# Two feed-forwards in split FP32: TensorE's written order at a part's end, and two adaLN steps moved behind up

## The chip, the cores and the metric

One core of one Trainium2 chip runs the whole program. The metric is the device time of one execution in microseconds. TensorE (PE; its weight loads are PEld) multiplies into PSUM; VectorE (DVE) and ScalarE (ACT) move and change data; GpSimd (POOL) adds and issues some of the DMAs; SyncE (SP) issues the others.

## The reference, cut to what matters

The model is one step of two layers over 640 tokens (512 latent, 128 context) of width 1024. Each layer has a token mixer (attention, then a recurrent unit) and a SwiGLU feed-forward of inner width 2816 = 22 x 128. The shift, scale and gate vectors of both (adaLN) come from a conditioning vector.

```python
def _swiglu(x, w_gu, w_down):
    gate, up = jnp.split(x @ w_gu, 2, axis=-1)
    return (jax.nn.silu(gate) * up) @ w_down

# per layer, after the mixer
f_l = _swiglu(_modulate(lat, norm_g[i, 1], sh2_l, sc2_l), ffn_w_gu[i], ffn_w_down[i])
lat = lat + g2_l[:, None, :] * f_l
```

## The kernel before

Activations lie with the feature on the partitions and the tokens along them, in eight 128-row tiles. Every FP32 operand is split into a high part (rounded, a ScalarE cast) and a low part (the rest, a VectorE subtraction), and a product is three matmuls for each 128-row tile: high x high, high x low, low x high. A planner orders the instructions of each engine: it simulates the program and gives an engine the earliest written instruction that it takes to be ready. `issue_after` puts an instruction behind another one of its engine, and `in_order` makes the chosen engines follow the written order inside its block; instructions from outside may still stand between.

The first feed-forward (`ffn`) works the 22 column blocks f in three parts of 8, 7 and 7. For each f, `ws` makes gate and then up, each in two chunks of tokens (24 matmuls a chunk). Gate's evacuation is L916 and a Silu, up's is L924, a bias step (L927) and the split into `hhi` and `hlo`. A part ends with its down projection (`project`): chunks of 3 matmuls for each f of the part, accumulated over f, and L595 adds each into x. Between, `fill` runs steps of `modulations`, which compute the adaLN vectors of later stages: one step loads 512 KB on POOL's queue (L288) and makes two VectorE products with accumulation (L292), each issued behind the last `self.anchor`. A quota of 56 steps holds for this phase: each gate and each up asks for one (not at f = 0), each chunk pair of the first two down projections for one more. `keep` loads later weights on POOL's queue too, splits them and stores them.

The second feed-forward works on blocks of 4 x 128 features and halves of 320 tokens, with a Strassen-like scheme: seven products for each pair f (gate and up block f) in place of eight, of 12 matmuls each. In the rows they are known by their operands:

- `pair_a(f)`: A11 x B11 (`mx<-big,whi`), copied by ScalarE to `snap`; then A12 x B21 (`mm<-big,whi`).
- `pair_b(f)`: S2 x T2 into the same mx bank (`mx<-big,whx`), copied to `snap` as u2; S1 x T1 (`mc<-big,whx`); S3 x T3 again into the mx bank, which has to wait for u2, and is copied as u3.
- `pair_c(f)`: A22 x T4 into the mx bank (`mx<-xt,wuh`), behind the copy u3; S4 x B22 into the mc bank (`mc<-big,whx`). Then `hidden` multiplies gate and up and splits the result.

`opening` ends the layer before, makes the first two pairs plainly (L1008) and the sums T1 to T4 and their halves (`sums`, `lows`: L1032, L1037) on VectorE, all in written order. `ffn_halves` then goes through six parts of 3, 3, 4, 4, 4 and 4 pairs; the first part's first two pairs are the opening's. The loop writes pair_a(f), pair_c(f - 1), pair_b(f). At a part's end it writes pair_a of the next part's first pair, pair_c, and the down projection (`project_part`), whose weights pass through the same three `raw` and three `whi` buffers as the gate weights. `gate_weights` loads and splits the gate block, `sum_weights` makes S1 to S4 on GpSimd and splits them.

Of the kernel before, what the change touches and what calls it, by code (L numbers as in the profile page):

```python
# [23 lines left out]
CHB = ((320, 642), (0, 320))  # L24
# [4 lines left out]
NF = FF // P  # L29
# [7 lines left out]
ORDERED = (mybir.EngineType.PE, mybir.EngineType.DVE, mybir.EngineType.Activation)  # L37
C0 = 516
FG = (1, 1, 1)
# [95 lines left out]
def _pieces(t0, t1):  # L135
    return [(s, max(a, t0), min(b, t1)) for s, a, b in ((0, 0, NLAT), (1, NLAT, NTOK)) if max(a, t0) < min(b, t1)]


class _Step:
# [761 lines left out]
    def ffn(self, l, hi, lo, fp, last):  # L901
        nc = self.nc
        f0 = 0
        todo = [k for f in range(KT) for k in [("wi", f + KT), ("wi", f)] + [("wg", f // 2)] * (1 - f % 2)] + [("wlo", f) for f in range(KT)]
        todo += [("gu", c * NF + f) for f in range(PLAIN) for c in range(2)] + [("gu", PLAIN)]
        for ci, n in enumerate((8, 7, 7)):
            hhi = self.big()
            hlo = self.big()
            sg = {}

            def eg(j):
                def ev(t0, s, ps):
                    if t0:
                        sg[j] = self.t([P, NTOK], F32, "sg", 2, fp)
                    g = sg[j]
                    self.anchor = nc.vector.tensor_tensor(g[:, s], ps, self.rt[:, s], ALU.mult).ins  # L916
                    for c, a, b in _pieces(s.start, s.stop):
                        nc.scalar.activation(g[:, a:b], g[:, a:b], AF.Silu, bias=self.bias[:, c:c + 1])
                return ev

            def eu(j):
                def ev(t0, s, ps):
                    u = self.t([P, 320], F32, "up", 2, fp)
                    nc.vector.tensor_tensor(u, ps, self.rt[:, s], ALU.mult)  # L924
                    for c, a, b in _pieces(s.start, s.stop):
                        g = sg[j][:, a:b]
                        nc.vector.scalar_tensor_tensor(g, u[:, a - t0:b - t0], self.bias[:, c:c + 1], g, ALU.add, ALU.mult)  # L927
                    self.mark = self.split(hhi[:, j, s], hlo[:, j, s], sg[j][:, s])
                    self.anchor = self.mark[1]
                return ev  # L930
            for j in range(n):
                f = f0 + j
                self.ws(self.i["gu"][l, f], hi, lo, eg(j), FG[0] * (f > 0), CHB)
                self.ws(self.i["gu"][l, NF + f], hi, lo, eu(j), FG[1] * (f > 0), CHB)
                self.keep(todo, KEEP[ci][j])
            w = self.i["dn"][l, :, :, f0:f0 + n]
            if ci == 2:
                last(w, hhi, hlo, (l, 5))
            else:
                def between(f, n=DOWN[ci]):  # L940
                    self.fill(FG[2])
                    self.keep(todo, n[f])
                self.project(w, hhi, hlo, (l, 5), done=between)
            f0 += n
# [307 lines left out]
    def ffn_halves(self, l, q):  # L1252
        self.wx, self.share = 0, False
        qs = [None] * PLAIN + [q]
        f0 = 0
        for ci, n in enumerate(CHN):
            for j in range(n):
                f = f0 + j
                if f < PLAIN:
                    continue  # L1260
                if f == len(qs):
                    qs.append(self.gate_weights(l, f))
                    self.pair_a(qs[f])
                if j and f > PLAIN:
                    self.sum_weights(qs[f])
                    self.pair_c(qs[f - 1])
                    self.last_weights(qs[f])
                self.pair_b(qs[f], j)
            w = self.i["dn"][l, :, :, f0:f0 + n]
            f0 += n  # L1270
            if f0 < NF:
                qs.append(self.gate_weights(l, f0))
                self.pair_a(qs[f0])
            self.pair_c(qs[f])
            if f0 == NF:
                self.share = True
                self.project_last(w, self.hhi, self.hlo, (l, 5))
            else:
                self.sum_weights(qs[f0], ci == 0)
                self.last_weights(qs[f0])  # L1280
                self.project_part(w, self.hhi, self.hlo, (l, 5))
# [398 lines left out]
```

## Time and profile before

| | |
|---|---|
| median of 3 runs | 1485.97 us (1485.88 to 1487.15) |
| the profiled execution | 1488.96 us, span 1487.1 |
| mean granted TensorE clock | 0.996 |
| busy: PE, DVE, ACT, POOL | 1471.2, 1075.0, 728.3, 247.9 us |
| first feed-forward, about | 370 to 840 us |
| second feed-forward, about | 1035 to 1480 us |

The span runs from the first to the last instruction. A busy TensorE is not TensorE at its peak: a matmul of 320 columns shows as 0.31 us, while the next one starts 0.147 us after it, so that two overlap. What counts for the time is the distance from start to start.

### The profile page before, as it was taken

The page shows a single profiled execution, that of the slowest core. Times are in us where ns is not written, and L with a number is a line of the kernel's source. Part 1 is how long each engine was busy: PE and PEld are TensorE (multiplying, and loading weights), DVE is VectorE, ACT ScalarE, POOL GpSimd, SP SyncE. Part 2 cuts the span into 40 slices and gives each one's busy share as a digit, 9 for nine tenths or more (in the row PEclk, how much of TensorE's full clock was granted, in tenths as well). Part 3 has the DMA queues.
Part 4 walks back from the last instruction along what each step waited for, and adds up shares of the span by engine and source line. Part 5 has one row for each costly group of instructions (what it writes and reads, how often), then busy time and mean ns, then how long its engine had stood idle before and what let it go on. Part 6 is the DMA issues. An engine that isn't in the chain of part 4 may idle for free.

```text
span 1487.1 us, 26372 instructions
## 1 busy us (share of the span) xinstructions
PE 1471.2 (99%) x10377; PEld 1440.2 (97%) x10377; DVE 1075.0 (72%) x2054; ACT 728.3 (49%) x1345; POOL 247.9 (17%) x325
## 2 busy tenths in 40 slices
PE   9999999999999999999999999999999999999997
PEld 5999999999999999999999999999999999999997
DVE  6788887875678788887876489985865666565545
ACT  5676666754333234322434298864634343424344
POOL 0001000000012222211210001112032322222311
PEclk9999999999999999999999999999999999999999
DMA  9555555443359899886863744267242131313121
GB/s 371 179 151 172 170 151 155 126 157 100 114 177 323 299 358 326 305 264 218 306 221 125 252 142 142 86 236 247 81 132 86 57 114 57 114 57 109 52 68 71
DMA packets 86026, 255.35 MB, mean 172 GB/s; under 512 B 9056, under 2 KB 22544, under 8 KB 85776
## 3 DMA queue, kind: packets, MB, share of 16 engines
q1 hardware_dynamic: 59152, 157.06, 32.3%
q0 software_dynamic: 26576, 96.49, 18.8%
q8 instruction: 81, 1.33, 0.4%
q14 instruction: 41, 0.34, 0.1%
q10 hardware_dynamic: 176, 0.13, 0.0%
HBM read 206.18 MB, written 43.53 MB: 168 GB/s over the span
## 4 chain that ended last, share of the span: by engine, by line
PE 79%; DMA 8%; DVE 5%; issue 3%; ACT 3%; POOL 1%; DVEq 0%; ACTq 0%; POOLq 0%
PE mm L253 11%; PE mm L255 11%; PE mm L254 11%; PE mx L253 4%; PE mx L255 4%; PE mx L254 4%; PE mx L1203 3%; PE mx L1204 3%; PE mx L1205 3%; DMA mraw<-in_wm 2%; PE op L888 2%; PE gp L1412 2%; PE tp L806 2%; PE mc L1204 1%; PE mc L1203 1%
## 5 line engine op out<-in xcount | busy, mean ns | idle before, releaser
L253 PE MATMUL mm<-big,whi 128*128 128x320 f32 (+3 forms) x1010 | 311.0, 311 | 1.9 <-ACT big L1529 1.8
L254 PE MATMUL mm<-big,whi 128*128 128x320 f32 (+3 forms) x1010 | 312.7, 310 | 0.3 <-DVE big L1530 0.3
L255 PE MATMUL mm<-big,wlo 128*128 128x320 f32 (+3 forms) x1010 | 312.2, 310 | 0.0
L292 DVE SCALAR_TENSOR_TENSOR mprod<-mraw,csb 128x1024 f32<-128x1024 f32 x160 | 194.7, 1217 | 19.6 <-DMA mraw<-in_wm 19.4
L253 PEld LDWEIGHTS mm<-big,whi 128*128 128x128 f32 x1010 | 189.6, 189 | 4.0 <-ACT big L1529 2.4
L254 PEld LDWEIGHTS mm<-big,whi 128*128 128x128 f32 x1010 | 190.5, 189 | 1.7 <-DVE big L1530 0.5
L255 PEld LDWEIGHTS mm<-big,wlo 128*128 128x128 f32 x1010 | 190.1, 189 | 1.0
L1529 ACT CAST whi<-raw 128x1024 fp32r<-128x1024 f32 (+2 forms) x103 | 105.3, 1024 | 143.7 <-PE mm L254 89.6
L1530 DVE TENSOR_TENSOR wlo<-raw,whi 128x1024 fp32r<-128x1024 f32 (+2 forms) x103 | 127.4, 1238 | 33.4 <-ACT whi L1529 33.1
L254 PE MATMUL mm<-big,whx 128*128 128x320 f32 (+3 forms) x443 | 137.4, 310 | 0.0
L255 PE MATMUL mm<-big,wlx 128*128 128x320 f32 (+3 forms) x443 | 137.2, 310 | 0.0
L253 PE MATMUL mm<-big,whx 128*128 128x320 f32 (+3 forms) x443 | 137.0, 310 | 0.0
L595 DVE SCALAR_TENSOR_TENSOR x<-mm,G,x 128x320 f32<-128x320 f32 (+3 forms) x202 | 81.1, 435 | 55.9 <-PE mm L255 50.7
L253 PE MATMUL mx<-big,whi 128*128 128x320 f32 (+3 forms) x318 | 99.2, 312 | 0.0
L255 PE MATMUL mx<-big,wlo 128*128 128x320 f32 (+3 forms) x318 | 98.6, 310 | 0.0
L254 PE MATMUL mx<-big,whi 128*128 128x320 f32 (+3 forms) x318 | 98.4, 310 | 0.0
L288 POOL DMA_DIRECT2D mraw<-in_wm x80 | 42.9, 536 | 317.1 <-DVE mprod L292 203.9
L255 PEld LDWEIGHTS mm<-big,wlx 128*128 128x128 f32 x443 | 83.6, 189 | 0.0
L254 PEld LDWEIGHTS mm<-big,whx 128*128 128x128 f32 x443 | 83.5, 189 | 0.0
L253 PEld LDWEIGHTS mm<-big,whx 128*128 128x128 f32 x443 | 83.4, 188 | 0.0
L1530 DVE TENSOR_TENSOR wlx<-sum,whx 128x1024 fp32r<-128x1024 f32 x40 | 50.2, 1254 | 38.5 <-ACT whx L1529 38.5
L218 ACT CAST kwh<-mraw 128x1024 fp32r<-128x1024 f32 x33 | 34.7, 1051 | 75.6 <-DMA kwi<-kwh 27.7
(396 smaller groups left out, 3886.5 us busy)
## 6 DMA issues: line engine op xcount, KB each, us to landing
raw<-in_gu SPq DMA_DIRECT2D x84, 512.0 KB, 3.6
mraw<-in_wm POOLq DMA_DIRECT2D x80, 512.0 KB, 5.3
raw<-in_dn SPq DMA_DIRECT2D x24, 512.0 KB, 3.7
sw<-in_wm SPq DMA_DIRECT2D x16, 512.0 KB, 10.1
raw<-in_wqk SPq DMA_DIRECT2D x16, 512.0 KB, 4.4
mraw<-in_wi POOLq DMA_DIRECT2D x16, 512.0 KB, 6.4
kwi<-kwh POOLq DMA_DIRECT2D x16, 512.0 KB, 6.3
kwi<-kwl POOLq DMA_DIRECT2D x16, 512.0 KB, 5.4
```

The costliest lines, as they stand in the source:

```text
L218: nc.scalar.copy(high, raw)
L253: nc.tensor.matmul(ps, hi[:, k], xhi[:, k, s], start=(k == 0), stop=False)
L254: nc.tensor.matmul(ps, hi[:, k], xlo[:, k, s], start=False, stop=False)
L255: nc.tensor.matmul(ps, lo[:, k], xhi[:, k, s], start=False, stop=(k == nk - 1))
L288: nc.gpsimd.dma_start(w, self.i["wm"][l * 6 + j - 2, f])
L292: nc.vector.scalar_tensor_tensor(prod, w, 1.0, self.csb[:, s], ALU.mult, ALU.mult, accum_out=out[:, s, f:f + 1])
L595: last = self.nc.vector.scalar_tensor_tensor(xs, ps[:, a - t0:b - t0], G[:, s, f:f + 1], xs, ALU.mult, ALU.add).ins
L1203: nc.tensor.matmul(ps, hi[:, k], xh[:, k], start=start and k == 0, stop=False, skip_group_check=not start)
L1204: nc.tensor.matmul(ps, hi[:, k], xl[:, k], start=False, stop=False, skip_group_check=not start)
L1205: nc.tensor.matmul(ps, lo[:, k], xh[:, k], start=False, stop=(k == KH - 1), skip_group_check=not start)
L1529: high = self.nc.scalar.copy(hi, v).ins
L1530: return high, self.nc.vector.tensor_tensor(lo, v, hi.bitcast(F32), ALU.subtract).ins
```

## The change

In the first feed-forward, the last pair of a part (j == n - 1) asks for no adaLN step after gate and for two after up. In the second one, a part's last pair_b, the next part's first pair_a and the last pair_c are written in this order under `in_order` for TensorE alone, and `gate_weights` of the next part is written ahead of that pair_b.

```diff
             for j in range(n):
                 f = f0 + j
-                self.ws(self.i["gu"][l, f], hi, lo, eg(j), FG[0] * (f > 0), CHB)
-                self.ws(self.i["gu"][l, NF + f], hi, lo, eu(j), FG[1] * (f > 0), CHB)
+                self.ws(self.i["gu"][l, f], hi, lo, eg(j), FG[0] * (f > 0 and j < n - 1), CHB)
+                self.ws(self.i["gu"][l, NF + f], hi, lo, eu(j), (FG[1] + FG[0] * (j == n - 1)) * (f > 0), CHB)
                 self.keep(todo, KEEP[ci][j])
...
                     self.pair_c(qs[f - 1])
                     self.last_weights(qs[f])
-                self.pair_b(qs[f], j)
+                if j < n - 1:
+                    self.pair_b(qs[f], j)
             w = self.i["dn"][l, :, :, f0:f0 + n]
             f0 += n
             if f0 < NF:
                 qs.append(self.gate_weights(l, f0))
-                self.pair_a(qs[f0])
-            self.pair_c(qs[f])
+            with self.in_order(ORDERED[:1]):
+                self.pair_b(qs[f], j)
+                if f0 < NF:
+                    self.pair_a(qs[f0])
+                self.pair_c(qs[f])
             if f0 == NF:
                 self.share = True
                 self.project_last(w, self.hhi, self.hlo, (l, 5))
```

## Rows read from the trace of the kernel before

**Rows 1.** The page: the span, and TensorE's busy time, share and instructions.

```profile
span 1487.1 us, 26372 instructions
PE 1471.2 (99%) x10377; PEld 1440.2 (97%) x10377; DVE 1075.0 (72%) x2054; ACT 728.3 (49%) x1345; POOL 247.9 (17%) x325
```

**Rows 2.** TensorE's waits: line, releaser, us in total, times, longest.

```profile
PE mm L253 <- ACT big L1529: 1.8, 2, 1.4
PE mx L1203 <- ACT snap L1209: 1.4, 3, 0.5
```

**Rows 3.** Timeline of VectorE, first feed-forward, end of part two: start, us, instruction.

```profile
632.96 0.48 DVE L916 TENSOR_TENSOR sg<-mm,r 128x320 f32<-128x320 f32 x1
...
634.36 1.21 DVE L292 SCALAR_TENSOR_TENSOR mprod<-mraw,csb 128x1024 f32<-128x1024 f32 x1
...
635.51 0.48 DVE L924 TENSOR_TENSOR up<-mm,r 128x320 f32<-128x320 f32 x1
635.91 1.21 DVE L292 SCALAR_TENSOR_TENSOR mprod<-mraw,csb 128x1024 f32<-128x1024 f32 x1
...
637.05 0.67 DVE L927 SCALAR_TENSOR_TENSOR sg<-up,bias,sg 128x192 f32<-128x192 f32 x2
```

**Rows 4.** Timeline of TensorE there: idle before it and what ended it, in brackets.

```profile
638.27 0.41 PE L253 MATMUL mm<-big,whi 128*128 128x320 f32 x1 [1.38 <-ACT big L1529]
```

**Rows 5.** Timeline of TensorE, second feed-forward, first part's end (f = 2).

```profile
1070.39 0.31 PE L1008 MATMUL mm<-big,whi 128*128 128x320 f32 x1
...
1074.94 0.31 PE L1203 MATMUL mm<-big,whi 128*128 128x320 f32 x1
...
1078.27 0.41 PE L1203 MATMUL mx<-big,whx 128*128 128x320 f32 x1 [0.52 <-ACT snap L1209]
...
1080.81 0.41 PE L1203 MATMUL mx<-xt,wuh 128*128 128x320 f32 x1 [0.52 <-ACT snap L1209]
...
1082.67 0.31 PE L1203 MATMUL mc<-big,whx 128*128 128x320 f32 x1
```

**Rows 6.** Timeline of VectorE there: the last low halves of T2, then T3.

```profile
1076.35 0.48 DVE L1037 TENSOR_TENSOR big<-c,big 128x320 fp32r<-128x320 f32 x1
1076.76 0.48 DVE L1037 TENSOR_TENSOR big<-x,big 128x320 fp32r<-128x320 f32 x1
```

**Rows 7.** Timeline of TensorE, fourth part's end: first matmuls from S3(12) to S3(13).

```profile
1275.07 0.31 PE L1203 MATMUL mx<-big,whx 128*128 128x320 f32 x1
...
1276.98 0.31 PE L1203 MATMUL mx<-big,whi 128*128 128x320 f32 x1
...
1280.20 0.31 PE L1203 MATMUL mx<-xt,wuh 128*128 128x320 f32 x1
...
1281.97 0.31 PE L1203 MATMUL mc<-big,whx 128*128 128x320 f32 x1
...
1283.73 0.31 PE L1203 MATMUL mx<-big,whx 128*128 128x320 f32 x1
...
1285.77 0.31 PE L253 MATMUL mm<-big,whi 128*128 128x320 f32 x1
...
1286.36 0.31 PE L1203 MATMUL mc<-big,whx 128*128 128x320 f32 x1
...
1288.86 0.31 PE L1203 MATMUL mx<-big,whx 128*128 128x320 f32 x1
```

**Rows 8.** Timeline of ScalarE there: the first down weight's cast, the copy of S2(13).

```profile
1283.69 1.05 ACT L1529 CAST whi<-raw 128x1024 fp32r<-128x1024 f32 x1 [0.54 <-DMA raw<-in_dn]
...
1285.97 0.41 ACT L1209 COPY snap<-mx 128x320 f32<-128x320 f32 x1
```

**Rows 9.** Timeline of TensorE, third part's end: A22(9).

```profile
1214.31 0.42 PE L1203 MATMUL mx<-xt,wuh 128*128 128x320 f32 x1 [0.35 <-ACT snap L1209]
```

**Rows 10.** Stretches near the start: busy time of each engine, granted clock, DMA.

```profile
10.00:15.00 5.00, 4.05 (x31) 2.13 (x30) 3.06 (x5) 1.88 (x4) 0.00 (x0) 1.00 1.03 419
15.00:20.00 5.00, 5.00 (x29) 4.00 (x26) 3.19 (x9) 1.32 (x2) 0.00 (x0) 0.52 1.02 415
20.00:25.00 5.00, 4.93 (x40) 2.97 (x39) 3.02 (x6) 3.82 (x10) 0.00 (x0) 0.80 1.03 410
```

## The prediction

> **What bounds the kernel now.** I read the page first: TensorE is busy for 1471.2 of 1487.1 us [rows 1], so a change that removes no product can gain only what TensorE waits, and loses whenever it makes TensorE wait. Then the table of TensorE's waits: the longest kind is 1.8 us in two waits for a ScalarE cast of `hhi` (first feed-forward), the next 1.4 us in three waits for `snap` (second feed-forward) [rows 2]. Idle under 0.15 us is not listed there. Then TensorE's timeline around each part's end. A wait costs more than the idle figure, because the profile lets a matmul last 0.31 us while the next starts 0.147 us later: twelve matmuls of one product take 1.76 us (1281.97 to 1283.73) [rows 7]. So an idle of 0.52 costs 0.52 + 0.16 = 0.68, and 0.8 with the slow first matmul after it (0.41 instead of 0.31) [rows 5].
>
> **First edit: the adaLN step of the last pair behind up.** A step is one load on POOL's queue and two VectorE products of 1.21 us. The quota of 56 is 14 + 8 + 14 + 8 + 12, so nothing is left for the last pair of the third part, and the edit moves two steps in all: f = 7 and f = 14. At f = 14 both products stand in VectorE's queue between gate and up, at 634.36 and 635.91; up's first evacuation starts at 635.51, and its bias step comes at 637.05 [rows 3]. ScalarE's cast follows that, and TensorE, which has the first six of the seven products of the down projection behind it, starts again at 638.27 after 1.38 us idle [rows 4]. Without the two products the bias step would come 2 x 1.15 = 2.3 us sooner (start to start 1.14 to 1.15), which is more than the wait. Saving: 1.38 + 0.16 = 1.5 us. What is late next: the two products now stand behind up's split, ahead of the residual steps of the down projection, which free PSUM banks; the three mm and two mx banks hold 5 x 3.1 us of chunks (21 matmuls each), so 2.3 us should drain unseen. The load buffer of the moved step comes free later, and with it the next load on POOL's queue, which also carries the weights that `keep` splits on VectorE. At f = 7 I saw no TensorE wait, so nothing to gain. Bounds: -1.7 (with the slow first matmul) to +1.5, if the late buffer makes a wait as long as the one removed. I take -1.5.
>
> **Second edit, at the first part's end (f = 2).** Before, the planner had worked pair_a(3) early: A12(3) starts at 1074.94, while VectorE still makes the low halves of T2 and T3 [rows 5, 6]. Then nothing is left to cover the copies: S3 waits at 1078.27 and A22 at 1080.81, 0.8 us each [rows 5]. In written order both waits go (S1 lies behind S2, pair_a behind S3): -1.6. But pair_a(3) may then no longer start before S3 is through, and S2, ahead of S3, ends only with T2's last low half, done at 1076.35 + 0.48 = 1076.83 (T3's is one instruction later) [rows 6]. Everything that must come after that moment: 2 matmuls of S2, 12 of S1, 12 of S3, 24 of pair_a, 24 of pair_c = 74 x 0.147 = 10.9 us, to 1087.7. Before, pair_c's second product starts at 1082.67 and ends 1.76 later, at 1084.43 [rows 5]. So TensorE ends this stretch 3.3 us later. Ahead of that moment it has only the last opening products (the last begins at 1070.39 [rows 5] and could begin sooner) and ten matmuls of S2; the rest is idle. The down weights cannot fill it: their three staging buffers hold gate and up weights until the sums are made. Bounds: -1.6 (only the waits go) to +3.3. I take +3.3, since the order of S3 and pair_a is forced, and the halves come from VectorE's chain, which the opening writes out and the change does not touch.
>
> **Second edit, parts two to five (f = 5, 9, 13, 17).** The sixth part has no next pair, and its products already stand in written order. At f = 13 I follow the rows. Before, pair_a(14) is not worked at the end of the part but one pair earlier: after S3(12) (1275.07) it starts at 1276.98 and fills the wait for the copy of S3(12) until A22(12) at 1280.20 [rows 7]. Now it is locked behind S3(13). What else could fill that place? pair_a(13) was used up earlier (one matmul is left), S2(13) comes only after the copies of S3(12) and A11(13), which ScalarE makes in that order, and the down weights are not cast before 1283.69 [rows 8]. So A22(12) waits for its copy, 0.8 us, as at 1080.81 [rows 5]. Then TensorE runs ahead, and meets the second limit: S3(13) needs the copy of S2(13), which stands in ScalarE's queue behind the cast of the first down weights, and that waits for its DMA; the copy starts at 1285.97 and takes 0.41 [rows 8]. So S3(13) cannot start before about 1286.45, wherever TensorE is. From the start of S3(12) that is 11.4 us, and the work in it is S3 12, one left over, A22, S4, S2 and S1 48 = 61 x 0.147 = 9.0 us. Loss 2.4 us. After S3(13), pair_a(14) covers the copy, and the chunks that filled in before (the first at 1285.77 [rows 7]) come later at no price. If down-weight chunks go ahead of S1 they wait for the same cast and give the same sum. The gain on the other side is the waits at A22 of the part's last pair: one of 0.35 idle, 0.5 us, at 1214.31 [rows 9]; the other ends show less than 0.15 idle, the f = 13 end none. Bounds for each part: 0 (something fills) to 2.4; 0.8 if only the copy is paid. I take 2.0, near the upper row, because ScalarE's queue is the same at all four, but some down-weight chunks may go in while S3 waits. Sum: 4 x 2.0 - 0.5 = +7.5.
>
> The emission of gate_weights ahead of pair_b moves one SP load and two casts; pair_b issues no DMA, so the order on SP's queue stays, and the next pair's gate weights were in use before. I count it at nothing, hidden by the products of the pair before; without that cover it is a cast of 1.05 us as at 1283.69 [rows 8] and a split.
>
> **A rule on the clock.** In the rows the granted clock averages 0.52 in 15 to 20 us and 0.80 in the next 5 us, that is half speed (1.2 of 2.4 GHz) for 5 x 0.48 + 5 x 0.20 = 3.4 us of lost full speed, after a stretch with TensorE's gaps and small products [rows 10]. The idle stretch that I expect ahead of 1076.83 is the only one in which this could happen again. The Trainium skill (TensorE: Matmul & The Clock Gate, section "Why this matters for your kernels") advises against idle gaps between bursts of matmuls in mid-kernel, since the clock then falls back to its half level. By that rule the sum would be 3.4 us more; the rows agree in kind, at the start of this kernel, and no run has yet shown it in mid-kernel.
>
> **Sum.** -1.5 + 3.3 + 7.5 = +9.3 us against the profiled execution, 1488.96 (span 1487.1 and 1.9 around it [rows 1]), which gives 1498.3. That execution lies 3.0 over the median of the runs, so beside that median: 1485.97 + 9.3 = 1495.3.
>
> **The rivals.** (a) The forecast, 1495: chance 0.48. (b) The change does what its words say: all waits go and nothing waits instead. -1.5 - 1.6 - 0.5 = -3.6, so 1482.4. It decides if other ready work stands where pair_a is taken away. For it: the waits exist [rows 2, 5, 9]; against it: at 1276.98 the planner took pair_a(14) because nothing nearer was ready, and at f = 2 the halves come late. Chance 0.2. (c) The lock costs only the copy: -1.5 + 3.3 + 4 x 0.8 - 0.5 = +4.5, so 1490.5; for it: the planner may put the copy of S2 ahead of the down weight's cast. Chance 0.2. (d) As (a), and the clock falls in the idle stretch: 1498.7, chance 0.12.
>
> About 0.2% (3 us) is what a measurement of this kernel tells from no change. A tenth of (b) falls inside it, and half of (c), where the first part's end turns out free as well (4.5 - 3.3 = 1.2): faster 0.2 - 0.02 = 0.18, same 0.02 + 0.10 = 0.12, slower the rest, 0.70. The range that leaves out (b) and little else is 1487 to 1500; the likeliest case alone, with its parts at 0.8 to 2.4, spans 1490 to 1498.
>
> **What would show it.** Right: at the end of the second part of the first feed-forward TensorE's 1.38 us are gone, and both VectorE products come behind up's split; TensorE idle for some us just before T2's last low half; pair_a of the next part between S3 and A22 of a part's last pair, without a wait; but a new wait of about 0.5 idle at A22 one pair earlier, and S3 of the last pair waiting for `snap`, behind the cast of a down weight. Wrong: if A22 one pair earlier follows S3 with other work between, or if the opening's products reach to T2's last half, the losses are not there and (b) holds.

## The result, and the profile after

The changed kernel takes 1494.59 us (median of 6 runs, 1493.11 to 1500.81) against 1486.36 for the kernel before (6 runs): a ratio of 1.0061, 95% interval 1.0044 to 1.0079, or 8.2 us slower. The forecast was 1495.3, range 1487 to 1500. The sum came out near; none of its three terms did, and their errors cancelled. (A ratio here need not be the quotient of two medians, which would be 1.0055.) The spans of the two traces differ by 5.0 only: the traced execution of before lies 2.6 over its median (1488.96 against 1486.36), that of the changed kernel 0.7 under (1493.93 against 1494.59).

The page of the changed kernel: span, and TensorE's busy time. It answers to [rows 1].

```profile
span 1492.1 us, 26383 instructions
PE 1471.8 (99%) x10377; PEld 1440.6 (97%) x10377; DVE 1074.6 (72%) x2054; ACT 732.6 (49%) x1345; POOL 249.2 (17%) x325
```

The work is the same; TensorE waits more. Its waits, as in [rows 2] (line, releaser, us in total, times, longest):

```profile
PE mx L1204 <- DVE big L1037: 3.4, 1, 3.4
...
PE mx L1203 <- ACT snap L1209: 1.3, 3, 0.4
...
PE mx L1203 <- ACT big L1033: 1.1, 1, 1.1
...
PE mc L1203 <- DVE g L1214: 0.9, 3, 0.3
```

The `snap` row was there before (three waits, two of them at the first part's end); now its three waits stand at the ends of parts three, four and five. The other three rows are new: one wait of 3.4 for a low half of T2, one of 1.1 for a high half, and three for `g`. The waits for `g` were in no part of the forecast.

**The first part's end.** TensorE's timeline there, which answers to [rows 5]: the last four matmuls of S2(2) (1069.28 to 1074.91), the first of S1(2), the fourth of S3(2), and the first of S4(2).

```profile
1069.28 0.31 PE L1205 MATMUL mx<-big,wlx 128*128 128x320 f32 x1
1070.66 0.42 PE L1203 MATMUL mx<-big,whx 128*128 128x320 f32 x1 [1.08 <-ACT big L1033]
1074.48 0.64 PE L1204 MATMUL mx<-big,whx 128*128 128x320 f32 x1 [3.40 <-DVE big L1037]
1074.91 0.47 PE L1205 MATMUL mx<-big,wlx 128*128 128x320 f32 x1
...
1075.18 0.47 PE L1203 MATMUL mc<-big,whx 128*128 128x320 f32 x1
...
1079.18 0.34 PE L1203 MATMUL mx<-big,whx 128*128 128x320 f32 x1
...
1086.10 0.31 PE L1203 MATMUL mc<-big,whx 128*128 128x320 f32 x1
```

From start to start the two waits cost 1.23 and 3.67 beyond 0.147, together 4.9; the two `snap` waits that are gone cost 1.6, so the stretch loses 3.3, the forecast's number. But the matmuls behind the idle stretch last 0.47, not 0.31: from 1074.48 to 1079.18 there are 17 steps in 4.70 us, where 17 x 0.147 is 2.5. That is 2.2 more. The windows say why (length, busy time and count of PE, PEld, DVE, ACT and POOL, granted TensorE clock, DMA share, GB/s):

```profile
1070.00:1075.00 5.00, 0.94 (x3) 0.71 (x4) 3.53 (x8) 2.81 (x6) 0.00 (x0) 0.74 0.29 111
1075.00:1080.00 5.00, 5.00 (x23) 5.00 (x22) 1.94 (x4) 0.89 (x2) 3.31 (x3) 0.58 0.69 218
```

The granted clock fell to its half level (1.2 of 2.4 GHz) before the idle stretch was over (0.74 on average from 1070 to 1075), and the matmuls are back at full speed from 1079.2 on; in the trace of before it was 1.00 in every window from 1060 to 1085. What held T2's half is in the chain of waits (start, us, what):

```profile
1070.15 0.86 ACT big L1033 x2
1071.01 0.40 ACT xt L1033
1071.41 0.96 ACT whx L1533
1072.39 1.23 DVE wlx L1534
1073.62 0.82 DVE big L1037 x2
1074.48 0.64 PE mx L1204
```

VectorE had written order here: the split of S3 and S4 (L1534), which waits for ScalarE's cast, stands ahead of the last four low halves. Before, it stood there too, but nothing on TensorE waited for it. T2's half came where the forecast had put it: this trace runs 2.4 us ahead of the one of before at this place (the last of the sums, L1032, starts at 1070.44 here and at 1072.85 there), and the half is done at 1074.43 against 1076.83.

**The fourth part's end**, answering to [rows 7]: first matmuls of S3(12), A22(12), S1(13), S3(13), pair_a(14), A22(13).

```profile
1277.90 0.31 PE L1203 MATMUL mx<-big,whx 128*128 128x320 f32 x1
...
1280.39 0.41 PE L1203 MATMUL mx<-xt,wuh 128*128 128x320 f32 x1 [0.43 <-ACT snap L1209]
...
1286.24 0.42 PE L1203 MATMUL mc<-big,whx 128*128 128x320 f32 x1 [0.29 <-DVE g L1214]
...
1288.11 0.31 PE L1203 MATMUL mx<-big,whx 128*128 128x320 f32 x1
...
1289.88 0.31 PE L1203 MATMUL mx<-big,whi 128*128 128x320 f32 x1
...
1293.97 0.32 PE L1203 MATMUL mx<-xt,wuh 128*128 128x320 f32 x1
```

pair_a(14) now covers the copy of S3(13), as the change says. One pair earlier A22(12) waits for its copy (0.43 idle, 0.7 with the slow matmul), and S1(13) waits 0.29 (0.55) for the addition that reads S4(12)'s bank (L1214): ten matmuls of S2(13) had gone ahead of S4(12), so only two stood between S4(12) and S1(13). The same two waits stand at f = 9 and 17, not at f = 5. S3(13) waits for nothing, because ScalarE's queue differs from [rows 8]; its timeline:

```profile
1286.56 0.42 ACT L1209 COPY snap<-mx 128x320 f32<-128x320 f32 x1
1286.88 1.05 ACT L1533 CAST whi<-raw 128x1024 fp32r<-128x1024 f32 x1
```

The copy of S2(13) now stands ahead of the first down weight's cast. The forecast had it behind, as before.

**The first feed-forward.** VectorE at the second part's end, answering to [rows 3]: up's evacuation, its bias step, the split, and only then an adaLN product.

```profile
630.34 0.49 DVE L924 TENSOR_TENSOR up<-mm,r 128x320 f32<-128x320 f32 x1
630.86 0.68 DVE L927 SCALAR_TENSOR_TENSOR sg<-up,bias,sg 128x192 f32<-128x192 f32 x2
...
634.83 0.49 DVE L1534 TENSOR_TENSOR big<-sg,big 128x320 fp32r<-128x320 f32 x1
635.24 1.22 DVE L292 SCALAR_TENSOR_TENSOR mprod<-mraw,csb 128x1024 f32<-128x1024 f32 x1
```

TensorE does not wait there in this trace. Why it does not is taken up under e5.

### The profile page after: what moved, and what is told of

Same layout as the page of the kernel before. It is cut to its first block, busy times and chain, and to the rows that moved or that the text cites. A ratio compares the mean times of both kernels' runs of the same rounds, so it can differ in the third digit from the quotient of the medians.

```text
span 1492.1 us, 26383 instructions
## 1 busy us (share of the span) xinstructions
PE 1471.8 (99%) x10377; PEld 1440.6 (97%) x10377; DVE 1074.6 (72%) x2054; ACT 732.6 (49%) x1345; POOL 249.2 (17%) x325
## 4 chain that ended last, share of the span: by engine, by line
PE 92%; DVE 3%; DMA 2%; ACT 2%; issue 1%; SPq 0%; DVEq 0%; ACTq 0%
PE mm L253 14%; PE mm L255 14%; PE mm L254 14%; PE mx L253 5%; PE mx L255 5%; PE mx L254 5%; PE mx L1203 3%; PE mx L1204 3%; PE mx L1205 3%; PE op L888 2%; DMA sw<-in_wm 2%; PE gp L1416 2%; PE tp L806 2%; PE mc L1203 2%; PE mc L1205 2%; PE mc L1204 2%
## 5 line engine op out<-in xcount | busy, mean ns | idle before, releaser
L1534 DVE TENSOR_TENSOR wlo<-raw,whi 128x1024 fp32r<-128x1024 f32 (+2 forms) x103 | 124.8, 1213 | 36.4 <-ACT whi L1533 36.0
L1534 DVE TENSOR_TENSOR wlx<-sum,whx 128x1024 fp32r<-128x1024 f32 x40 | 50.0, 1250 | 31.6 <-ACT whx L1533 31.6
L255 PE MATMUL mx<-big,wlx 128*128 128x320 f32 (+3 forms) x229 | 70.9, 310 | 0.0
## 6 DMA issues: line engine op xcount, KB each, us to landing
sw<-in_wm SPq DMA_DIRECT2D x16, 512.0 KB, 10.9
```

What stands on the lines that cost most here:

```text
L255: nc.tensor.matmul(ps, lo[:, k], xhi[:, k, s], start=False, stop=(k == nk - 1))
L1534: return high, self.nc.vector.tensor_tensor(lo, v, hi.bitcast(F32), ALU.subtract).ins
```

## The experiments

Each was timed beside the kernel before on its chip. Medians of before lay at 1487.4 to 1488.1 there, so the ratios compare.

| | ratio | 95% interval | median, us |
|---|---|---|---|
| changed kernel | 1.0061 | 1.0044 to 1.0079 | 1494.59 |
| e1 first edit alone | 1.0002 | 0.9991 to 1.0013 | 1487.50 |
| e2 first part's end alone | 1.0036 | 1.0023 to 1.0049 | 1492.72 |
| e3 the other ends alone | 1.0020 | 1.0012 to 1.0029 | 1490.68 |
| e4 idle filled | 1.0037 | 1.0025 to 1.0050 | 1492.57 |
| e5 before again | 0.9997 | 0.9983 to 1.0011 | 1487.74 |
| e6 pair_a(3) ahead | 1.0019 | 1.0008 to 1.0030 | 1491.55 |
| e7 pair_a not bound | 0.9988 | 0.9979 to 0.9996 | 1485.34 |
| e8 all pairs in one order | 1.0053 | 1.0041 to 1.0065 | 1496.09 |
| e9 changed kernel again | 1.0052 | 1.0040 to 1.0064 | 1495.51 |
| e10 written ahead only | 0.9987 | 0.9977 to 0.9998 | 1485.65 |
| e11 low halves first | 1.0016 | 1.0005 to 1.0027 | 1491.53 |
| e12 three small moves | 0.9972 | 0.9959 to 0.9985 | 1484.10 |

**e1: the first edit alone.** The kernel before with the two lines of the first feed-forward changed.

> The first edit alone. If the 1.38 us of idle (1.65 from start to start, with the slow matmul behind it) are simply gone, as in the trace of the changed kernel, the time is 1486.4 - 1.65 = 1484.7. Rival: the late products or loads give it back elsewhere, then 1486.4.

No gain was measured, although its trace shows no wait at the second part's end. So the wait itself was in question.

**e5: the kernel before, once more.**

> The kernel before once more, for a second trace of it and as a control of the timing (ratio 1.000). The first edit alone brought nothing in the timed runs, though the 1.38 us of idle that it was to remove stood in the trace of before. Theory: that idle belongs to the one profiled execution, in which the loads on POOL's queue ran some 4 us late; then it is under 0.5 here. Rival: it is in every execution, and the first edit gives it back elsewhere; then 1.4 again.

The theory failed: the wait was there again, longer. TensorE's timeline of this second trace, then its windows, then VectorE's and ScalarE's timelines just ahead:

```profile
639.15 0.41 PE L253 MATMUL mm<-big,whi 128*128 128x320 f32 x1 [2.23 <-ACT big L1529]
```

```profile
640.00:645.00 5.00, 5.00 (x26) 5.00 (x25) 5.00 (x11) 1.40 (x2) 0.53 (x1) 0.68 0.80 296
```

```profile
631.55 1.22 DVE L219 TENSOR_TENSOR kwl<-mraw,kwh 128x1024 fp32r<-128x1024 f32 x1 [1.81 <-ACT kwh L218]
```

```profile
630.47 1.05 ACT L218 CAST kwh<-mraw 128x1024 fp32r<-128x1024 f32 x1 [1.71 <-DMA mraw<-in_wlo]
```

The clock fell to its half level behind this wait as well (0.68 from 640 to 645). Its size is not fixed: VectorE is late because a step of `keep` (L219) waits for a cast, and that for a load on POOL's queue, which was issued at 622.85 here and at 621.12 in e10, where TensorE waited least. In the four traces without the first edit (before, e5, e10, e12) TensorE was idle there for 1.38, 2.23, 0.22 and 2.00 us. In the ten with it, eight show none; e6 shows 0.46 and e8 1.32 in two pieces. But the wait goes with the moment of that load. In the eight it was issued at 616.2 to 620.3, in e6 and e8 at 621.9 and 622.9, and without the edit at 621.1 to 624.9. Where the moments are alike, the edit takes off some 0.9 us of idle (2.23 in e5 against 1.32 in e8, 1.38 in before against 0.46 in e6). What it would take off behind an early load no trace shows, nor whether the edit itself brings the load forward. The timed executions show no gain: e1 has 1.0002, and e7 and e10, in which TensorE has the same order all through the second feed-forward and which differ by this edit and the block, 0.9988 and 0.9987. Whether the wait is smaller in executions without a profile, or the edit gives something back elsewhere, stays open.

**e2 and e3: the second edit, split by place.** Both are the changed kernel with the new order under a condition (`ci == 0` for e2, `ci > 0` for e3), first edit in:

```diff
-                if j < n - 1:
+                if j < n - 1 or not (ci == 0):
                     self.pair_b(qs[f], j)
...
-            with self.in_order(ORDERED[:1]):
-                self.pair_b(qs[f], j)
+            with self.in_order(ORDERED[:1]) if ci == 0 else nullcontext():
+                if ci == 0:
+                    self.pair_b(qs[f], j)
```

> The changed kernel with the new order at the first part's end (f = 2) alone. The trace of the changed kernel says 4.9 us of idle before S2's end and 2.3 us of matmuls at half clock, against 1.6 us of waits before, and one later wait of 0.66 less: 1486.4 - 1.65 + 5.6 - 0.7 = 1489.7. The forecast's own term (+3.3, no fall of the clock) gives 1488.1. If the loss sat at the other ends, it is 1484 to 1485.

> The changed kernel with the new order at parts two to five alone, the first part's end as before. The trace of the changed kernel says two waits of 0.69 and 0.56 us at three ends, +3.7, and some 1.7 us of former waits gone: 1486.4 - 1.65 + 2.0 = 1486.8. The forecast's own term (+7.5) gives 1492.3; if the new order only removed waits, 1483 to 1484.5.

Over e1 the first part's end costs 1492.7 - 1487.5 = 5.2 us and the other ends 1490.7 - 1487.5 = 3.2; together 8.4, against 8.2 for the whole. Each of the two differences is good to some 2 to 2.5 us, so the agreement is closer than it had to be. In e3 the two waits stand at all four ends, in the changed kernel at three, so its own share of the 3.2 may be some 1.2 less (0.7 + 0.55). Those at f = 5 in e3, on TensorE's timeline:

```profile
1124.67 0.41 PE L1203 MATMUL mx<-xt,wuh 128*128 128x320 f32 x1 [0.57 <-ACT snap L1209]
...
1130.52 0.41 PE L1203 MATMUL mc<-big,whx 128*128 128x320 f32 x1 [0.29 <-DVE g L1214]
```

**e4: the idle stretch filled.** The changed kernel with 32 extra matmuls at the first part's end, between the ninth and tenth matmul of S2(2); S1(2) starts its bank anew, so their product is dropped.

```diff
         for k in range(KH):
+            if k == KH - 1:
+                for e in range(extra):
+                    nc.tensor.matmul(spare, hi[:, e % 3], xh[:, e % 3], start=e == 0, stop=e == extra - 1)
...
-                self.pair_b(qs[f], j)
+                self.pair_b(qs[f], j, 32 * (ci == 0))
```

> The changed kernel with 32 more matmuls, of operands that are ready, in the first part's end where TensorE is idle (behind the ninth matmul of S2, into the bank that S1 then begins anew). If the half clock that follows the idle stretch is what costs 2.3 us there, these vanish: 1494.6 - 2.3 = 1492.3, with S1 at 0.147 us a matmul. If the stretch of slow matmuls has another cause, they stay at 0.267 and the time is 1494.6 or more.

Windows of its trace:

```profile
1070.00:1075.00 5.00, 5.00 (x36) 5.00 (x36) 3.49 (x7) 3.19 (x6) 0.00 (x0) 1.00 0.40 131
1075.00:1080.00 5.00, 4.98 (x34) 4.72 (x34) 3.05 (x7) 1.19 (x3) 3.34 (x3) 1.00 0.56 184
```

With more work, and T2's half no sooner, the kernel is faster: 1.0037 against 1.0061 and, in e9, 1.0052, some 2 to 3.5 us. These intervals overlap a little, so the time alone would not settle it. The trace does: the clock stays at 1.00, and S1(2) goes at 0.147 a matmul. The fall of the clock is shown, and the time agrees with the 2.2 us that the trace of the changed kernel gives for it. Nor does it look like a matter of the profiled executions alone: the mean granted clock of all executions averages 0.9958 for the changed kernel and 0.9952 in e9, but 0.9970 here, 0.9979 in e11, and 0.9973 to 0.9978 for the kernel before beside the experiments.

**e9: the changed kernel again.**

> The changed kernel once more, beside the kernel of the next experiment on one chip, and for a second trace. If the idle stretch before S2(2)'s end and the half clock behind it belong to the change and not to one execution, the trace shows both again (4.9 us of idle, some 17 matmuls at 0.267 us), and the ratio is 1.006; if the clock fell in that one execution only, the matmuls are at 0.147 and the ratio is 1.0045.

The idle stretch and the half clock were both there again (1.04 and 3.40 idle; 0.50 granted from 1075 to 1080). This time 21 steps took 5.77 us, 2.7 more than at full speed. They belong to the change.

**e11: T2's last half sooner.** In the opening, two lines exchanged:

```diff
-            self.s_split(q, 1)
             lows(3)
+            self.s_split(q, 1)
```

> The changed kernel with two lines of the opening exchanged: the last four low halves, T2's among them, ahead of the split of S3 and S4, for whose cast they wait on VectorE in the trace (1.47 us of idle and 1.15 us of split before them). If the moment of T2's last half sets the end of S2(2), as the forecast said, the idle there falls from 4.9 to about 2.2 us: 2.6 off, ratio about 1.004, and up to 2.3 more off if the clock then stays up (1.0025). If something else holds S2(2), nothing changes (1.0055).

TensorE's timeline and windows of its trace:

```profile
1070.37 0.42 PE L1203 MATMUL mx<-big,whx 128*128 128x320 f32 x1 [1.03 <-ACT big L1033]
1071.48 0.42 PE L1204 MATMUL mx<-big,whx 128*128 128x320 f32 x1 [0.70 <-DVE big L1037]
```

```profile
1070.00:1075.00 5.00, 3.94 (x25) 3.71 (x26) 4.47 (x10) 3.37 (x7) 2.70 (x2) 1.00 0.63 220
1075.00:1080.00 5.00, 5.00 (x36) 5.00 (x36) 1.97 (x3) 1.17 (x3) 1.76 (x2) 1.00 0.57 158
```

The wait for T2's half goes from 3.40 to 0.70, 2.7 less, and the clock stays up. The ratio is 1.0016, some 5 to 7 us under the changed kernel. So T2's last half did set the end of S2(2), and what held that half was the written order on VectorE.

**e6: pair_a(3) ahead of S2(2).** The edit of e2, with pair_a(3) written first inside the ordered block.

> The first part's end alone, in written order, but with pair_a(3) written ahead of S2(2) and not behind S3(2). If the place of pair_a(3) is what costs the idle stretch, its 24 matmuls fill 3.5 of the 4.9 us of idle, the clock stays up, and one wait of 0.8 at A22(2) comes back: some 0.5 over the first edit alone, 1488. If the order of S2, S1 and S3 costs it by itself, the idle and the half clock stay, and the time is 1492 as with the whole edit there.

TensorE's timeline and ScalarE's, there:

```profile
1075.59 0.42 PE L1204 MATMUL mx<-big,whx 128*128 128x320 f32 x1 [1.22 <-DVE big L1037]
...
1082.03 0.41 PE L253 MATMUL mm<-big,whi 128*128 128x320 f32 x1 [2.35 <-ACT whi L1534]
```

```profile
1081.15 0.83 ACT L1534 CAST whi<-raw 128x768 fp32r<-128x768 f32 x1 [3.31 <-DMA raw<-in_dn]
```

The idle ahead of T2's half falls from 4.5 to 1.2, as the first theory said. But with pair_a(3) gone from behind S3(2), the planner put six down-weight matmuls there, and their weight had not landed. The clock fell again (0.86 and 0.80 in the next two windows of 5 us). The time lies between the two expectations and settles neither; the rows do.

**e7 and e10: pair_a written ahead, not bound.** e7 is e3 with pair_a outside the block; e10 has neither the block nor the first edit:

```diff
-                self.pair_b(qs[f], j)
+                if j < n - 1 or ci == 0:
+                    self.pair_b(qs[f], j)
...
                 self.pair_a(qs[f0])
+            if ci > 0:
+                self.pair_b(qs[f], j)
             self.pair_c(qs[f])
```

> Parts two to five alone, with S2, S1, S3, A22 and S4 of the last pair in written order, and pair_a of the next part written ahead and not bound to them. If the wait at A22 one pair earlier comes from binding pair_a behind S3, it is gone at all four ends, and the time is that of the first edit alone, 1487.5, or up to 1 less. If binding the last pair's five products costs by itself, it is 1489 to 1491.

> The kernel before with one thing changed: at the ends of parts two to five gate_weights and pair_a of the next part are written ahead of the last pair_b. No binding, no first edit. If the gain of the unbound version comes from the written place alone, the ratio is 0.9985 to 0.999, as there (1485.3 against 1487.9), and the waits at A22(5), A22(9) and A22(17) are gone; if the first edit had a share in it, the ratio is 0.9995 or more, and 1.4 us or more of idle stand at the second part's end of the first feed-forward.

Both are faster than before. In both traces TensorE waits for no `snap` and no `g` at any of the four ends; only the two `snap` waits of the first part are left. The binding of the last pair's products adds nothing: without it, in e10, TensorE has the same order from the first matmul of the second feed-forward to the last. From e3 to e7 the only difference is pair_a: bound behind S3, or written ahead of the last pair_b and free. It is worth some 5 us (1490.7 - 1485.3, each beside its own kernel before). The gain over the kernel before, about 2 us, comes from the written place alone, of gate_weights and pair_a together; gate_weights by itself was not tried.

**e8: every pair in one order.** From part two on, all products chained, with a `tail` that is kept from block to block:

```diff
...
+                with self.chain(ci):
+                    self.pair_a(qs[f])
...
+                with self.chain(ci):
+                    self.pair_c(qs[f - 1])
...
+                with self.chain(ci):
+                    self.pair_b(qs[f], j)
```

> From part two on every product of every pair in one written order (S3, A11, A12, A22, S4, S2, S1, S3 of the next, and so on), down-weight chunks free to stand between; first part as before; first edit in. Every copy then has 24 matmuls, and every g a whole S2, in front of its reader, so the waits at A22 and S1 (two at each end in the changed kernel) and those of the kernel before (some 2 us in parts two to five) should all go: 1485 to 1486. Rival: the chunks, now in lumps of up to 48 and 65 matmuls, wait for their weights or for the residual steps that free their banks, and the gain is eaten: 1487.5 or more.

It is as slow as the change. ScalarE's timeline at the third part's end, and TensorE's S3(9):

```profile
1208.50 1.05 ACT L1534 CAST whi<-raw 128x1024 fp32r<-128x1024 f32 x1 [2.53 <-DMA raw<-in_dn]
...
1210.77 0.41 ACT L1209 COPY snap<-mx 128x320 f32<-128x320 f32 x1
```

```profile
1211.23 0.41 PE L1203 MATMUL mx<-big,whx 128*128 128x320 f32 x1 [1.00 <-ACT snap L1209]
```

Here the copy does stand behind the cast of a down weight that waits for its DMA, and S3 waits for it, again at f = 13 and 17 (1.09 and 1.06). This is the second limit of the forecast, in a kernel where the queue has that order. The longest single wait of e8 is another one: S1 waits 1.68 for `g` at 1122.73, which stands on VectorE behind the split of a weight that ScalarE casts late. The rival named chunks that wait for weights or residual steps; its sign was right, but the waits are at the products.

**e12: three small moves together.** e10, the exchange of e11, and at the first part's end the order A11(3), S2, S1, S3, A12(3), A22, S4:

```diff
...
+            with self.in_order(ORDERED[:1]) if ci == 0 else nullcontext():
+                if ci == 0:
+                    a11 = self.pair_a(qs[f0], False, True)
+                self.pair_b(qs[f], j)
+                if ci == 0:
+                    self.pair_a12(qs[f0], a11)
+                self.pair_c(qs[f])
```

> The kernel before with pair_a of the next part written ahead of the last pair_b at parts two to five (as in the moved version, 0.9987), the last low halves ahead of the split of S3 and S4, and at the first part's end the written order A11(3), S2, S1, S3, A12(3), A22, S4. S1 and A12(3) then cover the two copies for which TensorE waited 0.8 us each, and T2's last half is there 2.6 us sooner, so nothing idles ahead of it: 1.6 less than the moved version, ratio 0.9977. Rival: S3 then waits for the split that was put back, or a chunk for its weights, and the ratio stays 0.9987 or more.

It is the fastest of all, 4 us under the kernel before. TensorE's timeline: the second part's end of the first feed-forward, and the only idle over 0.15 us at the first part's end.

```profile
640.87 0.41 PE L253 MATMUL mm<-big,whi 128*128 128x320 f32 x1 [2.00 <-ACT big L1544]
```

```profile
1076.79 0.41 PE L1204 MATMUL mx<-big,whx 128*128 128x320 f32 x1 [0.27 <-DVE big L1037]
```

## Why the prediction was right, and where it was not

- **First edit, -1.5.** The wait was gone from the trace, as the forecast said, but not shown to be gone for its reason: the load on POOL's queue, which the forecast did not price, was early there. Where it was late (e6, e8), the wait stayed in part. The size failed too. It was read from one execution, 3.0 over the median of the runs, and the forecast took the wait as part of every run. Measured: 0, interval -1.3 to +1.9.
- **First part's end, +3.3.** The wait was right in mechanism and size: 4.9 lost against 1.6 of former waits. The whole term was not. From T2's last half (1074.43) to S4(2)'s end (1086.10 + 12 x 0.147 = 1087.86) it is 13.4 us: the forecast's 10.9, 2.2 for the half clock, and 0.3 for two down-weight matmuls. The step that fell short is the clock, which stood in rival (d) and not in the sum: measured at this place, 5.2 in time. That VectorE's chain is fixed by written order was right; that it could be reordered (e11) was not seen.
- **Parts two to five, +7.5.** Over-sized. The first limit came as described, at three of the four ends: A22 one pair earlier waits for its copy, 0.7 against the 0.8 that was priced. The second did not: the forecast carried ScalarE's order from the trace of before into a kernel whose planner chose another one, which was the condition of rival (c). In its place came a wait of S1 for S4's bank, 0.55, which the forecast lacked. Former waits gone were priced at 0.5; at the A22 of the last pairs the trace of before has 0.13, 0.35 and 0.10 idle, together some 1.4 from start to start. Measured: 3.2, in e3.
- **The rule on the clock.** The granted clock fell in mid-kernel in or behind idle stretches, in both traces of the changed kernel, in e2, in e5 and in e6, and it stayed up where the stretch was filled (e4) or shortened (e11), and behind the 2.00 us of e12. The Trainium skill (TensorE: Matmul & The Clock Gate, section "Why this matters for your kernels") warns of such gaps between bursts; the traces agree, at 2.2 us for this one and 2.7 in e9. The forecast had put 3.4, from the start of one execution; the same stretch of the changed kernel's trace shows no fall at all, as the window below says, which answers to [rows 10]. The first part's end was also not the only place where the clock could fall: e5 is the kernel before, and it fell there at 640.

```profile
15.00:20.00 5.00, 4.89 (x46) 3.41 (x39) 4.10 (x12) 3.01 (x7) 0.00 (x0) 1.00 1.03 418
```

- **The total.** 0 + 5.2 + 3.2 = 8.4, against 9.3 forecast and 8.2 measured. What happened is nearest to (c) with (d)'s clock, not (a). The sum came out by luck: a loss over-sized by 4.3 stood against a saving of 1.5 that was not there and 1.9 at the first part's end, where the fall of the clock had been left out.

## What to carry to other kernels

Where a planner orders the queues, a trace tells what waited under the old order, not the order of the queues after an edit: price each wait from the dependence itself and treat the old queue as one of the cases. Binding a product behind another takes it away from every earlier place where it was filling a wait, so look one step earlier; writing it sooner and leaving it free can give the gain without the loss (e7, e10). A wait read from a single execution is a sample: before pricing its removal, ask what made it late.

## What the runs showed that was not expected

- The same wait at the second part's end of the first feed-forward was 0.22 to 2.23 us long in four traces of kernels that have the same instructions there, and once, at 2.23, it took the clock down with it; at 2.00 it did not.
- 32 useless matmuls made the changed kernel some 2 to 3.5 us faster; with them the granted clock stayed at 1.00.
- After idle of 1.08 and 3.40 us the matmuls went at half the clock for 17 steps in one trace, and after 1.04 and 3.40 for 21 in another; with 1.03 and 0.70 it stayed at 1.00.
